# First MLP chunk's second product in seven half-size products, and three changes of order in a transformer block on one core

## The chip, the cores and the metric

The kernel runs on one core of one Trainium2 chip. Its time is device time in microseconds (us). TensorE does the matrix products and writes PSUM; VectorE, ScalarE and GpSimd do the element-wise work; SyncE and GpSimd issue the transfers that are told of here. The profile is one execution taken by the hardware profiler. In it PE is TensorE's matmuls, PEld its weight loads, DVE is VectorE, ACT is ScalarE, POOL is GpSimd, SP is SyncE. [...]

## The reference

One encoder block over 1024 tokens (a grid of 16 rows of 64) and 1024 features, in float32:

```
n = RMSNorm(h);  proj = n @ w_in               (columns: attention q, k, v; GLA q, k, v, r, z)
A = 2-D neighbourhood attention, 8 heads of 64, window 8 x 16, with a bias by relative position
B = bidirectional gated linear attention (GLA), 4 heads, in chunks of 64 tokens; each head's
    output is RMS-normalised and gated by silu(r)
h = h + concat(A, B) @ w_out
h = h + square(relu(RMSNorm(h) @ w1)) @ w2     (w1: 1024 x 4096, w2: 4096 x 1024)
out = RMSNorm(h)
```

## The kernel before, in words

**Layout and parts.** Activations are held with features on the 128 partitions and tokens along the free axis. A float32 product is made of three matmuls: each operand is split into a high part (a cast on ScalarE, `S.copy` to the type float32r) and a low part (the operand less its high part: `low`, line 1057, a subtraction on VectorE or GpSimd), and high x high, high x low and low x high are added up in a PSUM bank of 128x512. Matmuls go out in the order of the program, through `PE`, whose `keep_in_program_order` is at line 115.

**Order of the other engines.** Outside the MLP a scheduler orders the instructions of VectorE, ScalarE and GpSimd by its own estimates and by priorities (`tc.high_priority`), except those kept in program order. In the MLP nearly every instruction is kept in program order (`kp`).

**GLA (lines 440 to 695).** The four heads h = 0 to 3 run one after the other. Between their steps TensorE does the projections of later blocks as filling work: `fill.at(GLA_FILL, h, i)` runs so many steps of three matmuls each. For each half of the 16 token chunks, `gla_contrib` makes eight 64x128 products in two PSUM banks with the tag "s" and copies them to `st`: upper state rows (partitions 0 to 63, line 583) and lower ones (64 to 127, line 586), all four copies of a half on ScalarE. `gla_scan` then runs the recurrence over the chunks on VectorE, forwards on the upper partitions and backwards on the lower ones, one instruction for each step and direction. `gla_within` makes the products inside chunks in two more "s" banks, whose results VectorE copies under a mask (line 600). `gla_intra` and `gla_inter` add up the head's output in a bank "o". `gla_norm` squares it, sums over features with a matmul by ones (bank "t"), and `rstd_from` takes the inverse root with four instructions of ScalarE and two of VectorE; two more of VectorE multiply by the gate and by the output into `yg`. The scan of a head is cut in three: steps 1 to 7 before the first half's `gla_within`, 8 to 11 before the second half's, 12 to 14 behind it.

**Attention (from line 740).** `softmax(p, b, ...)` makes the scores of one pair of heads p and one block of tokens b in two "s" banks, reads them with the bias `bt` on VectorE (line 825), and takes the exponential on ScalarE (827), the reciprocal and the scaling on VectorE (829, 830). `turn` transposes the result on TensorE. The scores of block b + 1 are issued before the transposes of block b, so both banks "s" must have been read by then. `masked` adds masks to the bias on VectorE (771).

**MLP (from line 1040).** The 4096 hidden features are worked off in four chunks of 1024. Each chunk has a first product (w1) and a second (w2), and each product is a list of half-stages of 12 matmuls. `stage` appends half-stages to one list; `go_on` works it off, calling `prepare(k)` ahead of half-stage k. `prepare` issues, in this order: the additions that follow from half-stage k - 1 (`sums`), early sums, the second step of preparing k + 1 (`prep1`), the first step of preparing k + 2 (`prep2`: high and low parts of weights and inputs), late sums, the activation of half-stage k - 1 (`acts`), and the jobs set for k (`job`).

In chunks 1 and 2 both products (`First`, `Second`) are seven products of half-size matrices each, with sums and differences of quarters (Strassen's way in Winograd's form), thus 14 half-stages. Weight sums are called S1 to S4, input sums T1 to T4, quarters A11 to A22 of the weights and B11 to B22 of the inputs; which sums are made where stands in `KW`, `KB`, `FIRST_SUMS` and `SECOND_SUMS`. `Second` takes its inputs' low parts (`lows`) on GpSimd, each pair held back until a first matmul of the half-stage before has run.

In chunk 0 both products are plain: `FirstPlain` and `SecondPlain` have 16 half-stages each. Beside `FirstPlain`, jobs make the second half of the normed activations: `normed` forms a 128x512 block (line 1382) and `put` splits it (cast on ScalarE at 1371, low part on VectorE); the eight blocks come at half-stages 2 to 7. Then `sums123` makes T1 to T3 of the four feature blocks for chunk 1 at half-stages 8 to 15, in the order 1, 2, 3, 0, with GpSimd adding the parts of B11 (`whole`, line 1367), and `sum4` makes T4 in chunk 1. `Weights` loads four quarters of 512 KB on SyncE's queue into four buffers of the tag "raw", each when its buffer is free.

## Time and profile before

| | us |
|---|---|
| median of 3 runs | 1180.3 (1179.51 to 1181.38) |
| profiled execution | 1180.51 |
| its span, first to last instruction | 1178.6 |
| PE busy in the span | 1149.7 (98%) |
| DVE busy | 862.7 (73%) |
| ACT busy | 664.8 (56%) |
| POOL busy | 241.6 (21%) |

The granted clock is 0.990 on average over the span. A record's duration for a pipelined matmul is longer than the distance to the next one; the pace is read from runs of matmuls in the chain of waits. The same holds, less strongly, for VectorE and ScalarE, whose records overlap a little at their ends. In a row of a timeline the bracket gives the idle time ahead of the instruction and what ended it.

### The profile page before, as it was taken

The page shows a single profiled execution, that of the slowest core. Times are in us where ns is not written, and L with a number is a line of the kernel's source. Part 1 is how long each engine was busy: PE and PEld are TensorE (multiplying, and loading weights), DVE is VectorE, ACT ScalarE, POOL GpSimd, SP SyncE. Part 2 cuts the span into 40 slices and gives each one's busy share as a digit, 9 for nine tenths or more (in the row PEclk, how much of TensorE's full clock was granted, in tenths as well). Part 3 has the DMA queues.
Part 4 walks back from the last instruction along what each step waited for, and adds up shares of the span by engine and source line. Part 5 has one row for each costly group of instructions (what it writes and reads, how often), then busy time and mean ns, then how long its engine had stood idle before and what let it go on. Part 6 is the DMA issues. An engine that isn't in the chain of part 4 may idle for free.

```text
span 1178.6 us, 15430 instructions
## 1 busy us (share of the span) xinstructions
PE 1149.7 (98%) x5632; PEld 945.6 (80%) x5632; DVE 862.7 (73%) x1565; ACT 664.8 (56%) x1222; POOL 241.6 (21%) x199
## 2 busy tenths in 40 slices
PE   8999899999999999999999999999999999999996
PEld 8878788767887878887788888888888888888876
DVE  8777868766767785686858875967859768587455
ACT  6767566656666665455634636446355463453665
POOL 5200000202021123510003320402304114032005
PEclk8999999989999999999999999999999999999998
DMA  7333132322324252320211112111211122111204
GB/s 241 76 86 94 41 72 46 87 69 55 80 45 100 68 179 73 107 107 8 82 54 36 54 54 72 37 55 54 72 66 31 50 69 72 54 37 54 72 1 143
DMA packets 40283, 84.03 MB, mean 71 GB/s; under 512 B 9264, under 2 KB 20656, under 8 KB 40208
## 3 DMA queue, kind: packets, MB, share of 16 engines
q1 hardware_dynamic: 36608, 71.11, 18.1%
q0 software_dynamic: 3456, 11.94, 5.8%
q8 instruction: 44, 0.72, 0.2%
q14 instruction: 31, 0.25, 0.1%
q10 hardware_dynamic: 144, 0.00, 0.0%
HBM read 78.85 MB, written 5.96 MB: 72 GB/s over the span
## 4 chain that ended last, share of the span: by engine, by line
PE 83%; DVE 7%; ACT 6%; issue 1%; DMA 1%; SPq 0%; DVEq 0%; ACTq 0%
PE f L115 26%; PE u L115 24%; PE proj L115 15%; PE op L115 7%; PE sc L115 2%; PE no L115 2%; PE o L115 1%; PE pt L120 1%; PE sb L115 1%; PE ob L115 1%; PE z L115 1%; PE a L115 1%; DMA wl<-in_w_in 1%; PE c L115 1%; PE opl L115 0%
## 5 line engine op out<-in xcount | busy, mean ns | idle before, releaser
L1079 ACT CAST ph<-A 128x512 fp32r<-128x512 f32 x166 | 102.9, 621 | 146.5 <-PE f L115 73.6
L1057 POOL TENSOR_TENSOR ul<-uB,uh 128x512 fp32r<-128x512 f32 x84 | 109.1, 1317 | 330.5 <-ACT uh L1092 213.4
L115 PE MATMUL f<-uh,ph 128*128 128x512 f32 x400 | 155.9, 390 | 2.1 <-ACT u L1100 1.4
L115 PE MATMUL f<-ul,ph 128*128 128x512 f32 x400 | 155.8, 390 | 0.1
L115 PE MATMUL f<-uh,pl 128*128 128x512 f32 x400 | 155.8, 389 | 0.0
L1057 DVE TENSOR_TENSOR pl<-A,ph 128x512 fp32r<-128x512 f32 x166 | 112.7, 688 | 52.6 <-ACT ph L1079 52.6
L115 PE MATMUL proj<-nh,wh 128*128 128x512 f32 x352 | 151.1, 429 | 0.0
L115 PE MATMUL proj<-nh,wl 128*128 128x512 f32 x352 | 139.4, 396 | 1.4 <-DMA wl<-in_w_in 1.4
L115 PE MATMUL proj<-nl,wh 128*128 128x512 f32 x352 | 138.9, 395 | 0.0
L1239 DVE TENSOR_TENSOR hT<-hT,f 128x512 f32<-128x512 f32 x168 | 113.0, 687 | 19.8 <-PE f L115 19.6
L115 PEld LDWEIGHTS f<-uh,ph 128*128 128x128 f32 x400 | 75.1, 188 | 18.4 <-ACT u L1100 1.8
L115 PEld LDWEIGHTS f<-ul,ph 128*128 128x128 f32 x400 | 75.1, 188 | 16.0 <-DVE ul L1057 0.4
L115 PEld LDWEIGHTS f<-uh,pl 128*128 128x128 f32 x400 | 75.1, 188 | 15.6
L115 PE MATMUL u<-n,ph 128*128 128x512 f32 x288 | 85.2, 391 | 0.0
L115 PEld LDWEIGHTS proj<-nh,wh 128*128 128x128 f32 x352 | 67.2, 191 | 18.2 <-issue 5.6
L1092 ACT CAST uh<-uB 128x512 fp32r<-128x512 f32 x84 | 51.9, 618 | 51.1 <-PE f L115 33.0
L115 PEld LDWEIGHTS proj<-nh,wl 128*128 128x128 f32 x352 | 66.8, 190 | 16.9 <-DMA wl<-in_w_in 1.8
L115 PE MATMUL u<-T,ph 128*128 128x512 f32 x256 | 77.0, 390 | 0.2 <-ACT ph L1079 0.2
L115 PEld LDWEIGHTS proj<-nl,wh 128*128 128x128 f32 x352 | 67.2, 191 | 11.7 <-issue 1.7
L115 PE MATMUL op<-y,wh 128*128 128x512 f32 x240 | 75.6, 396 | 0.4 <-DVE y L714 0.4
L115 PE MATMUL u<-nt,ph 128*128 128x512 f32 x224 | 69.0, 389 | 0.0
L827 ACT ACTIVATE xsc<-xsc,sm 128x384 f32<-128x384 f32 (+1 forms) x64 | 37.3, 584 | 51.3 <-DVE sm L825 51.1
(302 smaller groups left out, 2469.6 us busy)
## 6 DMA issues: line engine op xcount, KB each, us to landing
A<-in_w SPq DMA_DIRECT2D x64, 512.0 KB
wf<-in_w_in SPq DMA_DIRECT2D x22, 512.0 KB
wl<-in_w_in POOLq DMA_DIRECT2D x21, 512.0 KB, 6.7
wf<-in_w_out SPq DMA_DIRECT2D x17, 512.0 KB
hT<-in_xT SPq DMA_DIRECT2D x2, 2048.0 KB
xs<-in_xT SPq DMA_DIRECT2D x6, 512.0 KB
out<-hT SPq DMA_DIRECT2D x4, 512.0 KB
out<-hT SPq DMA_DIRECT2D x8, 256.0 KB
```

Of the source, the lines that this page charges most:

```text
L115: m = nc.tensor.matmul(*args, **kw)
L120: tc.keep_in_program_order(nc.tensor.transpose(*args, **kw))
L827: S.activation(x[:, :n], x[:, :n], AF.Exp, scale=-1.0, bias=sm[:, i, 0:1], accum_out=sm[:, i, 1:2])
L1057: return kp(eng.tensor_tensor(l, x, h.bitcast(F32), op=ALU.subtract))
L1079: kp(S.copy(ph, x))
L1092: kp(S.copy(uh, x))
L1239: kp(V.tensor_tensor(hT[:, d, c], hT[:, d, c], o[:, s], op=ALU.add))
```

## The change: what it does

1. **Second product of chunk 0.** `SecondPlain` (16 half-stages) goes; chunk 0 uses `Second` as chunks 1 and 2 do (14 half-stages). So `FirstPlain` gets a `late` step that makes T1 (two subtractions on VectorE) and S3 (two weight sums) at its last half-stage. S1 is not made on VectorE: `sum_by_dma` loads A21 from memory into the tile "S" and adds A22 onto it with a second, accumulating transfer, both issued by GpSimd, set as a job at half-stage 9. The first two low parts of the second product's inputs go to VectorE (`eng=V`), without the gate.
2. **Order in the first product of chunk 0.** Low parts are no longer issued right behind their cast. `prep2` and `put` append them to the list `owed`, and `settle` works it off inside the next job, between two other VectorE instructions. The eight normed blocks come at half-stages 2 to 6, `sums123` at 7 to 14 in the order 0 to 3. T1 is formed by subtracting B11's high part and then its low part from B12 (two instructions on VectorE in place of one on GpSimd and one on VectorE), and T2 = B22 - T1.
3. **GLA.** The copies of the lower state rows (line 586) go from ScalarE to VectorE. The scan is cut at 8, 10 in place of 8, 12. For the last head's second half, `gla_norm` is taken apart: the matmul by ones stays where it was, the four ScalarE instructions are issued at the start of attention, and the four VectorE instructions behind the first softmax.

The core of the diff:

```diff
-                S.copy(st[64:128, n0 - 1 + 2 * k:n0 + 6:2, :], src[64:128, k:4, :])
+                V.tensor_copy(st[64:128, n0 - 1 + 2 * k:n0 + 6:2, :], src[64:128, k:4, :])
...
-            gla_scan(dec, st, NCH // 2, NCH - 4)
+            gla_scan(dec, st, NCH // 2, NCH // 2 + 2)
             fill.at(GLA_FILL, h, 4)
             gla_within(h, 1, qD, kI)
-            gla_scan(dec, st, NCH - 4, NCH - 1)
+            gla_scan(dec, st, NCH // 2 + 2, NCH - 1)
...
-            gla_norm(h, 1, ob[1], sq[1])
+            if h + 1 < GH:
+                gla_norm(h, 1, ob[1], sq[1])
+            else:
+                v_last = bank("t", "ovlast")
+                PE.matmul(v_last, ones, sq[1], start=True, stop=True)
+                o_last = ob[1]
...
+        ly = qp.tile([P, T], F32, tag="qc", name="ly")[:, 0:H]
+        lt, lu = qt(), qt()
+        S.activation(lt, v_last, AF.Ln, bias=epsb, scale=LNSH / P)
+        S.activation(ly, lt, AF.Exp, bias=expb, scale=-0.5)
+        S.activation(lu, v_last, AF.Identity, bias=epsn, scale=-0.5 / P)
+        S.activation(lt, ly, AF.Square)
         with tc.high_priority(offset=SOON_B):
             bt = bias_for(0)
         fill.run(NA_PRE)
         xs = softmax(0, 0, *qk, bt)
+        tc.keep_in_program_order(V.tensor_tensor(lt, lt, lu, op=ALU.mult))
+        V.scalar_tensor_tensor(ly, lt, 1.5, ly, op0=ALU.add, op1=ALU.mult)
+        c = slice(H, T)
+        V.tensor_tensor(ly, yg[GH - 1][:, c], ly, op=ALU.mult)
+        V.tensor_tensor(yg[GH - 1][:, c], ly, o_last, op=ALU.mult)
         masked(bt, (5, 0))
...
+        def sum_by_dma(self, dst, a, b, src):
+            self.t[dst] = t = mu.tile([P, D], F32, tag="S", name=dst)
+            kp(G.dma_start(t, src[("A11", "A12", "A21", "A22").index(a)]))
+            kp(G.dma_start(t, src[("A11", "A12", "A21", "A22").index(b)], accum_op=ALU.add))
...
     class FirstPlain(Stage):
+        def late(self, p, kh):
+            if p == (1, 3) and kh:
+                for i in range(2):
+                    t = self.u["B12", i]
+                    kp(V.tensor_tensor(t, t, self.u["B11", i], op=ALU.subtract))
+                for i in range(2):
+                    self.after.w.sum("S3", i)
...
-            self.parts[p, kh] = self.w.low(self.w.high(f"A{p[1] // 2 + 1}{kh + 1}", p[1] % 2))
+            ph, x = self.w.high(f"A{p[1] // 2 + 1}{kh + 1}", p[1] % 2)
+            pl = mp.tile([P, H], F32R, tag="pl", name="pl", bufs=3)
+            self.parts[p, kh] = ph, pl
+            if self.late_lows:
+                owed.append((pl, x, ph))
+            else:
+                low(pl, x, ph, V)
...
+        if isinstance(st, FirstPlain) and get(k + 1)[0] is not st:
+            for n in (k + 1, k + 2):
+                halves[n][0].lows(*halves[n][1:], eng=V)
...
     def put(key, k, x):
         h, l = place(key, k)
         kp(S.copy(h, x))
-        low(l, x, h, V)
+        owed.append((l, x, h))
+
+    def settle():
+        while owed:
+            low(*owed.pop(0), V)
...
         kp(V.scalar_tensor_tensor(t, hT[:, 4 * c + k, H:T], gff[:, 4 * c + k:4 * c + k + 1], r1,
                                   op0=ALU.mult, op1=ALU.mult))
+        settle()
         put(key, k, t)
...
+        h, l = place("B11", k)
         if step == 0:
-            b["B11", k] = ub("b11")
-            whole(b["B11", k], "B11", k)
+            x = ub("t3")
+            kp(V.tensor_tensor(x, b22, b12, op=ALU.subtract))
+            settle()
+            put("T3", k, x)
+            kp(V.tensor_tensor(b12, b12, h.bitcast(F32), op=ALU.subtract))
+        else:
+            kp(V.tensor_tensor(b12, b12, l.bitcast(F32), op=ALU.subtract))
+            settle()
+            put("T1", k, b12)
             kp(V.tensor_tensor(b22, b22, b12, op=ALU.subtract))
-            put("T3", k, b22)
-        else:
-            kp(V.tensor_tensor(b12, b12, b["B11", k], op=ALU.subtract))
-            kp(V.tensor_tensor(b22, b22, b["B11", k], op=ALU.add))
-            put("T1", k, b12)
+            settle()
             put("T2", k, b22)
...
-    f2 = SecondPlain(0, f1.u)
+    f1.after = f2 = Second(0, f1.u)
     stage(f2)
```

## Rows read from the trace of the kernel before

**Rows 1.** The page, parts 1 and 4: busy time by engine; the chain that ended last.

```profile
PE 1149.7 (98%) x5632; PEld 945.6 (80%) x5632; DVE 862.7 (73%) x1565; ACT 664.8 (56%) x1222; POOL 241.6 (21%) x199
...
PE 83%; DVE 7%; ACT 6%; issue 1%; DMA 1%; SPq 0%; DVEq 0%; ACTq 0%
```

**Rows 2.** The chain that ended last: start us, length us, what; x is instructions.

```profile
531.99 7.28 PE u L115 x32
...
582.87 39.09 PE f L115 x171
621.96 38.09 PE u L115 x168
660.05 38.08 PE f L115 x168
```

**Rows 3.** Who TensorE waited for, from 526 to 630 us: total, times, longest.

```profile
PE f L115 <- ACT u L1100: 1.4, 1, 1.4
PE u L115 <- ACT B L1371: 1.0, 1, 1.0
```

**Rows 4.** VectorE in order of time, first product: start us, length us, instructions [idle before].

```profile
535.94 1.29 DVE L1057 TENSOR_TENSOR pl<-A,ph 128x512 fp32r<-128x512 f32 x2
...
541.28 0.69 DVE L1057 TENSOR_TENSOR T<-b,T 128x512 fp32r<-128x512 f32 x1 [0.69 <-ACT T L1371]
541.89 0.75 DVE L1382 SCALAR_TENSOR_TENSOR b<-hT,gff,r 128x512 f32<-128x512 f32 x1
```

**Rows 5.** VectorE, then GpSimd, in order of time, from 725 to 745 us.

```profile
732.01 3.49 DVE L1074 TENSOR_TENSOR S<-A,A 128x512 f32<-128x512 f32 x2
...
737.23 0.68 DVE L1057 TENSOR_TENSOR pl<-A,ph 128x512 fp32r<-128x512 f32 x1
...
731.80 1.45 POOL L1057 TENSOR_TENSOR ul<-uB,uh 128x512 fp32r<-128x512 f32 x1 [38.46 <-ACT uh L1092]
```

**Rows 6.** DMA issues of the page's part 6: KB each, us to landing.

```profile
wl<-in_w_in POOLq DMA_DIRECT2D x21, 512.0 KB, 6.7
```

**Rows 7.** Who TensorE waited for, from 20 to 528 us.

```profile
PE a L115 <- ACT st L586: 1.7, 2, 1.1
...
PE la L115 <- DVE asb L600: 0.8, 1, 0.8
...
PE a L115 <- DVE asb L600: 0.5, 1, 0.5
```

**Rows 8.** Windows: length, busy (and instructions) by engine, granted clock, DMA share, GB/s.

```profile
110.00:160.00 50.00, 46.78 (x260) 37.09 (x260) 37.85 (x65) 31.37 (x49) 2.97 (x5) 0.97 0.30 70
126.00:132.00 6.00, 5.54 (x26) 4.31 (x26) 4.37 (x10) 0.91 (x2) 0.00 (x0) 0.72 0.62 168
256.00:264.00 8.00, 6.95 (x19) 4.87 (x20) 6.22 (x24) 4.82 (x12) 0.86 (x1) 0.57 0.48 93
```

**Rows 9.** VectorE, then TensorE, in order of time, from 236 to 290 us.

```profile
251.31 0.69 DVE L804 TENSOR_TENSOR vT<-proj,rms 128x512 f32<-128x512 f32 x1
252.91 0.69 DVE L239 TENSOR_TENSOR nt<-nt,nu 128x512 f32<-128x512 f32 x1 [0.91 <-ACT nt L238]
...
255.09 0.69 DVE L636 TENSOR_TENSOR yg<-ny,o 128x512 f32<-128x512 f32 x1
...
259.06 0.55 DVE L825 CUSTOM_DVE_ANT_0 xsc<-sc,bt 128x384 f32<-128x384 f32 x1
...
256.85 0.69 PE L115 MATMUL sc<-k00p,q 128*128 128x384 f32 x1 [2.67 <-DVE sm L825]
...
264.39 0.34 PE L115 MATMUL sc<-k00p,q 128*128 128x384 f32 x1
```

**Rows 10.** Groups by line: count, busy us, mean ns, idle before and its releaser.

```profile
L830 DVE TENSOR_SCALAR xsc<-xsc,sm 128x384 f32<-128x384 f32 (+1 forms) x64 | 26.2, 412 | 1.7
...
L888 DVE TENSOR_TENSOR yn<-no,otmp 64x512 f32<-64x512 f32 x16 | 10.9, 682 | 2.3 <-ACT otmp L885 1.8
...
L586 ACT COPY st<-c 64x512 f32<-64x512 f32 (+1 forms) x16 | 8.9, 555 | 0.2
```

More of the change, by code (lines that the diff above doesn't have):

```diff
@@ L692, in block_kernel @@
             fill.at(GLA_FILL, h, 10)
[L693 removed]
+            if h + 1 < GH:
[4 more added lines that the diff above has]
+                o_last = ob[1]
+                assert (h, 1) in gated
         bias_rows(range(ROWS))
@@ L1209, in prep1, with lows @@
                 self.pw[p, i] = self.w.low(self.hw[p, i])
-        def lows(self, p, i, gate=None):
-            self.pu[p, i], op = ulow(self.hu[p, i], G)
+        def lows(self, p, i, gate=None, eng=G):
+            self.pu[p, i], op = ulow(self.hu[p, i], eng)
             if gate is not None:
@@ L1239, in add @@
                 kp(V.tensor_tensor(hT[:, d, c], hT[:, d, c], o[:, s], op=ALU.add))
+    owed = []
     class FirstPlain(Stage):
         order = [((hf, m), kh) for hf in range(2) for m in range(4) for kh in range(2)]
+        late_lows = False
         def __init__(self, c):
             self.w, self.u, self.parts = Weights(w1[c], ("A11", "A12", "A21", "A22")), {}, {}
-        def prep2(self, p, kh):
-            self.parts[p, kh] = self.w.low(self.w.high(f"A{p[1] // 2 + 1}{kh + 1}", p[1] % 2))
+        def late(self, p, kh):
[5 more added lines that the diff above has]
+                    self.after.w.sum("S3", i)
+        def prep2(self, p, kh):
+            ph, x = self.w.high(f"A{p[1] // 2 + 1}{kh + 1}", p[1] % 2)
[5 more added lines that the diff above has]
+                low(pl, x, ph, V)
         def mm(self, p, kh):
@@ L1267, in acts @@
                 relu2(u, self.last)
-    class SecondPlain(Stage):
-        order = [((mh, k), hf) for mh in range(2) for k in range(4) for hf in range(2)]
-        def __init__(self, c, u):
-            self.w, self.u, self.b, self.parts = Weights(w2[c], ("A11", "A12", "A21", "A22")), u, {}, {}
-        def prep2(self, p, hf):
-            mh, k = p
-            if hf == 0:
-                self.wp = self.w.low(self.w.high(f"A{mh + 1}{k // 2 + 1}", k % 2))
-            uu, _ = ulow(uhigh(self.u[f"B{k // 2 + 1}{hf + 1}", k % 2]), V)
-            self.parts[p, hf] = self.wp + uu
-        def mm(self, p, hf):
-            wh, wl, uh, ul = self.parts.pop((p, hf))
-            mh, k = p
-            for j in range(4):
-                if k == 0:
-                    self.b[hf, j] = bank((("o", "t"), ("mm", "s"))[hf][j // 2], f"f{mh}_{hf}_{j}")
-                o = self.b[hf, j]
-                for n, (a, x) in enumerate(((wh, uh), (wl, uh), (wh, ul))):
-                    PE.matmul(o, a[:, j * P:(j + 1) * P], x, start=k == n == 0, stop=k == 3 and n == 2,
-                              skip_group_check=True)
-                if k == 3:
-                    c, d = slice(hf * H, (hf + 1) * H), mh * 4 + j
-                    kp(V.tensor_tensor(hT[:, d, c], hT[:, d, c], o, op=ALU.add))
     halves, jobs, at = [], {}, [0]
@@ L1331, in go_on @@
             else:
-                for t, q in lows:
-                    t.lows(*q)
+                if not isinstance(st, FirstPlain):
+                    for t, q in lows:
+                        t.lows(*q)
                 st.mm(p, i)
@@ L1400, in sum4 @@
         if step == 0:
+            settle()
             b["x", k] = x = [mp.tile([P, H], F32, tag=tag, name=f"b4{k}", bufs=3) for tag in ("uh", "ul")]
@@ L1407, in sum4 @@
             put("T4", k, x[0])
-    for n, k in enumerate((2, 3, 3, 4, 5, 5, 6, 7)):
+    f1.late_lows = True
+    for n, k in enumerate((2, 2, 3, 3, 4, 5, 5, 6)):
         job(k, normed, ("B12", "B22")[n // 4], n % 4)
-    for n, k in enumerate((1, 2, 3, 0)):
-        for step in range(2):
-            job(8 + 2 * n + step, sums123, k, step)
     for k in range(4):
         for step in range(2):
-            job(33 + 2 * k + step, sum4, k, step)
-    f2 = SecondPlain(0, f1.u)
+            job(7 + 2 * k + step, sums123, k, step)
+    job(15, settle)
+    job(9, lambda: f2.w.sum_by_dma("S1", "A21", "A22", w2[0]))
+    for k in range(4):
+        for step in range(2):
+            job(31 + 2 * k + step, sum4, k, step)
+    job(39, settle)
+    f1.after = f2 = Second(0, f1.u)
     stage(f2)
@@ L1421, in block_kernel @@
     stage(f1)
-    go_on(30)
+    go_on(28)
     for c in range(1, nchunk - 1):
```

## The prediction, made blind

> **What bounds the kernel now.** I read the page's busy times first, then the chain that ended last, then TensorE's waits, then the engines in order of time where it waited. TensorE is busy for 98% of the span and holds 83% of the chain [rows 1]. The chain shows its pace: in the MLP 168 matmuls of 512 columns take 38.08 us [rows 2], so one costs 38.08 / 168 = 0.2267 us (the longer durations of single records overlap), and a half-stage of 12 costs 2.72 us. From 621.96 us on, one such block follows the next without a gap. What can be gained is therefore matmuls taken out and waits of TensorE. The waits that this change touches stand in three places: the first MLP chunk [rows 3], the border between GLA and attention [rows 9], and the second GLA head [rows 7]. After the longer waits the granted clock was low as well: 0.57 on average in the 8 us behind the first and 0.72 in the 6 us behind the other [rows 8]. [...]
>
> **First chunk, TensorE.** The second product has 16 half-stages of 12 matmuls now and 14 afterwards: 24 x 0.2267 = 5.44 us less, on the engine that sets the end. The first product's second half-stage starts at 531.99 and the next chunk starts at 621.96 [rows 2]: 89.97 us for 15 + 16 = 31 half-stages, which need 31 x 2.72 = 84.3 us. So 5.6 us are waits, single ones up to 1.4 us [rows 3], the rest short.
>
> **First chunk, VectorE.** The waits come from a pattern. VectorE makes a normed block, ScalarE casts it, and VectorE stands idle for the cast (0.69 us) before it subtracts the low part; only then comes the next block [rows 4]. With the new order the low parts are owed and are done one job later, when their cast is over. I count VectorE's work anew. A 512-column operation costs 0.61 us start to start (two in a row 1.29, less one record of 0.68 [rows 4]), a normed block 0.75 less the same overlap of 0.08, 0.67 us.
> From 536.55 (the first of the pair at 535.94 [rows 4] is done): 8 normed blocks, 5 weight low parts and 7 low parts of the blocks, 8 x 0.67 + 12 x 0.61 = 12.7 us, so 549.2. TensorE needs the last of these at half-stage 9, at 531.99 + 8 x 2.72 = 553.8; now it waits there for the cast. Then, over half-stages 7 to 14: 16 sums, 8 weight low parts and 12 block low parts, 36 x 0.61 = 22.0 us, so 571.2, where TensorE stands at 570.1 (531.99 + 14 x 2.72). This is a balance: nine operations, 5.5 us, for each pair of half-stages of 5.44 us. TensorE waits for none of them, since the sums are for the next chunk and each weight low part comes a half-stage before its use.
> Half-stage 15 then puts seven operations on VectorE: the two first low parts of the second product (they stood on GpSimd in the later chunks), two T1 and two S3 sums, one owed low part, 4.3 us, so 575.5. The first needs of the second product are met (its low parts are done at 572.4, its start is 572.8). Its second half-stage needs a weight low part two operations later, at 576.7, and TensorE wants it with that half-stage's second matmul at 572.8 + 2.72 + 0.23 = 575.7: a wait of about 1.0 us. I take 0.7, since nothing in the count lets VectorE fall back further, and put 0 and 2 us as bounds. From there on it is the later chunks' stage, in which TensorE has no wait [rows 2]: VectorE's additions from PSUM rise from 16 to 28, 12 x 0.61 = 7.3 us more, and with 14 weight low parts and 10 weight and T sums they come to 52 x 0.61 = 31.7 us beside 38.1 us of matmuls.
> Moving those two low parts to VectorE costs 2 x 0.61 and spares a slower pairing: beside GpSimd's low part two weight sums took 3.49 us on VectorE in place of some 1.3 [rows 5].
> Sum for the chunk: 5.4 + 5.6 - 0.7 = **10.3 us** less. Bounds: 11.0 (no wait left) and 4.4 (all old waits stay, plus 1 us).
>
> **One weight sum by DMA.** Two transfers of 512 KB through GpSimd's queue, the second adding onto the first, so it must wait for it: by the rows of such transfers 2 x 6.7 [rows 6] = 13.4 us, a little more with issuing. They can start when the tile that holds block 0 of the normed halves is free, after its last low part at about 556.7, so S1 is there at about 571; ScalarE casts it at about 573 to 575. Behind these transfers on GpSimd stands only the third half-stage's low part, wanted after 575.5. I cost it at nothing. The weights' loads on SyncE's queue, in their new order, wait for the first product's buffers: the last is free at about 568 and, by the same 6.7 us, there at 574.5, before its sum S4 at about 578. If a transfer were late, ScalarE would hold its queue, and TensorE would wait as long.
>
> **Border of GLA and attention.** TensorE runs out at 254.2 and waits 2.67 us until softmax 0 has read its scores [rows 9]. VectorE stood before that in the last head's norm, whose four operations (252.91 to 255.7, after a wait of 0.91 for ScalarE) come ahead of the softmax. Afterwards softmax 0 comes first and can start at 251.9. So the wait at 256.85 goes. What is late next: the four operations now stand between softmax 0 and the masks and scores of softmax 1. VectorE's total to the end of those scores stays, less the idle 0.91 and the short idles around it: 260.0 becomes 259.1 to 259.9. TensorE reaches the third scores at full clock about 4.4 us after 254.2 (12 projection matmuls 2.7, scores 1.0, transposes 0.6), at 258.6, and waits about 1 us. In the trace these scores come at 264.39 [rows 9]: 4.9 us earlier. VectorE's idle time behind it is then used up, and I give back 0.7 us. **4.2 us** less. Bounds: 6.1 (the whole wait and the lost clock) and 0 (the new wait is as long and the clock falls again).
>
> **GLA.** The scan now does two steps rather than four between the halves, so the second half's masks stand four scan instructions earlier: the 0.8 us wait for them [rows 7] goes. Eight pairs of state copies go to VectorE for the lower partitions. On ScalarE each took 0.555 us [rows 10]; the trace has no such copy on VectorE. Nearest rows: 0.682 us (64x512 with an operand in PSUM) above, 0.412 (a scale in SBUF, 128x384) below [rows 10]; I take 0.65, nearest to the first. That is 16 x 0.65 = 10.4 us more for an engine busy 76% here [rows 8], beside 8.9 us less on ScalarE. In the second head TensorE waited 1.7 us for the last of four copies in a row [rows 7], which two engines now share, but a projection's evacuation ahead of them on VectorE moves back by the first pair, and ScalarE's copies behind it. I take half of that and nothing of the clock: 0.8 + 0.7 = **1.5 us** less. Bounds: 4.7 (all three waits, 3.0, and the clock, 1.7) and 3 us more (every head waits 0.75 for the longer VectorE queue).
> [...]
>
> **Sum.** 10.3 + 4.2 + 1.5 = 16.0 us off the profiled execution's 1180.5 (span 1178.6 and 1.9 around it), 1164.5; the median of the runs, 1180.3, is 0.2 below that execution, so 1164.3.
>
> **Rivals.**
> 1. *The border's wait moves, not shrinks.* VectorE has the same work before softmax 1; if TensorE again waits some 2.5 us there and the clock falls, the gain is 0: 1164.3 + 4.2 = 1168.5. For it: VectorE has under 1 us of idle there. Against: half a stage more of TensorE's work is issued before the wait.
> 2. *The first product is bound by VectorE.* Its balance has no slack; if each pair costs 0.7 us more (a cast late, S1 late, GpSimd's issuing in the way), all 5.6 us of waits come back: 1164.3 + 5.6 = 1169.9. That would be the change not doing what its order is for. For it: the count above. Against: no operation in the pair waits for a cast made in the same step.
> 3. *Slower: the GLA copies on VectorE.* The 10.4 us stand on the path of all four heads, whose scans feed the products, and each head's wait takes the clock down for as long as the second head's did, 1.7 us: 10.4 + 6.8 = 17.2 more in place of 1.5 less: 1164.3 + 18.7 = 1183.0. It decides from where VectorE ends a half's two copies later than TensorE has used up the filling projections. For it: VectorE is the busiest engine after TensorE. Against: heads one, three and four now show no wait of TensorE for VectorE or ScalarE above 0.8 us.
> 4. *Everything goes:* 11.0 + 6.1 + 4.7 = 21.8, 1158.5.
>
> **How the numbers follow.** Forecast, all three places gaining, 1160 to 1168: 0.53. Rival 1: 0.17, rival 2: 0.12, rival 3: 0.06, rival 4: 0.12. The range reaches to rivals 4 and 2 with their own spread: 1157.5 to 1173.0, leaving out rival 3 and the ends, about 0.15. A measurement of this kernel tells 0.2%, 2.4 us, from no change. Faster 0.93, same 0.02, slower 0.05: only rival 3 and a sum of two others reach the last two.
>
> **What would show it.** 24 fewer matmuls, and the chunk from 531.99 to the next one's start about 79.7 us long in place of 90.0; no TensorE wait over 1.1 us in it, and the one at the second half-stage of the second product named by a weight low part. No wait of TensorE on softmax 0, one near 1 us for softmax 1, and the clock at 1.00 behind it. VectorE copies near 0.65 us. I am wrong if attention's blocks begin no earlier, if TensorE waits in heads that had no wait, or if the chunk's first product keeps its waits.

## The result, and the profile after

The changed kernel takes 1167.39 us (median of 4 runs, 1167.19 to 1167.57), the kernel before, on the same chip, 1179.9: a ratio of 0.9894 with a 95% interval of 0.9882 to 0.9906, 12.5 us. Forecast were 1164.3 us in a range of 1157.5 to 1173.0, with the largest chance on 1160 to 1168. The profiled execution took 1167.57 us with a span of 1165.8, 12.8 us less than the span before.

First the page of the changed kernel, parts 1 and 4, to be set beside [rows 1]:

```profile
PE 1139.0 (98%) x5608; PEld 939.0 (81%) x5608; DVE 882.0 (76%) x1603; ACT 656.3 (56%) x1210; POOL 253.3 (22%) x209
...
PE 84%; DVE 7%; ACT 5%; DMA 2%; issue 1%; SPq 0%; DVEq 0%; ACTq 0%
```

There are 24 matmuls fewer, as forecast, and TensorE is still the bound. VectorE has 19 us more to do. The chain of waits shows where the MLP's stages begin now (compare [rows 2]):

```profile
527.39 35.39 PE u L115 x156
...
572.18 35.49 PE f L115 x155
607.67 21.77 PE u L115 x96
...
630.64 16.62 PE u L115 x72
647.26 38.08 PE f L115 x168
```

From 562.78 to 572.18 the chain follows VectorE, whose low part ends a wait of TensorE at 572.18. TensorE itself has no break before that wait: its waits in the first product, in [rows 3] before, are no longer listed, and the product's 180 matmuls behind 527.39 end at 568.20. The first chunk's second product ends at 607.67. The second chunk's first product, which was one block of 38.09 us before, is in two pieces with a gap at 629.44. The six largest of TensorE's waits between 40 and 720 us (total, times, longest; compare [rows 3, 7]):

```profile
PE proj L115 <- DMA wl<-in_w_in: 2.4, 2, 1.4
PE c L115 <- DVE st L586: 1.8, 2, 1.0
PE pt L120 <- DVE xsc L836: 1.2, 1, 1.2
PE u L115 <- ACT uB L1195: 1.2, 1, 1.2
PE a L115 <- DVE asb L600: 1.1, 1, 1.1
PE f L115 <- DVE pl L1075: 1.0, 1, 1.0
```

And two of the windows that [rows 8] showed (length, busy by engine, TensorE's granted clock as a share of full speed, DMA share, GB/s):

```profile
126.00:132.00 6.00, 5.24 (x32) 3.83 (x31) 5.62 (x14) 1.04 (x3) 0.40 (x1) 1.00 0.79 176
256.00:264.00 8.00, 6.09 (x30) 4.56 (x31) 6.45 (x20) 2.48 (x10) 0.00 (x0) 1.00 0.60 133
```

The granted clock is 1.00 in both, where before it was 0.72 and 0.57. To see where the 12.8 us are, I cut the span at the same instructions of TensorE in both traces: the first gate product of the first head (51.18 us before, 51.48 after), the last sum of squares of the GLA's outputs that both kernels have (243.21, 242.96), the scores of block 3 in attention (270.83, 266.42), the start of the first MLP product (528.28, 523.68), the start of chunk 1 (621.96, 607.67) and of its second product (660.05, 647.26).

| Stretch | before, us | after, us | gain | forecast |
|---|---|---|---|---|
| up to the first gate product | 51.18 | 51.48 | -0.30 | 0 |
| GLA, four heads | 192.03 | 191.48 | 0.55 | 1.5 |
| border to attention | 27.62 | 23.46 | 4.16 | 4.2 |
| attention and output projection | 257.45 | 257.26 | 0.19 | 0 |
| MLP chunk 0 | 93.68 | 83.99 | 9.69 | 10.3 |
| first product of chunk 1 | 38.09 | 39.59 | -1.50 | 0 |
| the rest | 518.55 | 518.54 | 0.01 | 0 |

The first row is code that all these kernels share; the transfer of the first input stands in it, and it moved between 50.72 and 51.48 us in the runs below. So a difference under 0.8 us between two whole profiled executions is no evidence; I use the lengths of stretches and the medians.

### The profile page after: what moved, and what is told of

Same layout as the page of the kernel before. It is cut to its first block, busy times and chain, and to the rows that moved or that the text cites. A ratio compares the mean times of both kernels' runs of the same rounds, so it can differ in the third digit from the quotient of the medians.

```text
span 1165.8 us, 15400 instructions
## 1 busy us (share of the span) xinstructions
PE 1139.0 (98%) x5608; PEld 939.0 (81%) x5608; DVE 882.0 (76%) x1603; ACT 656.3 (56%) x1210; POOL 253.3 (22%) x209
## 4 chain that ended last, share of the span: by engine, by line
PE 84%; DVE 7%; ACT 5%; DMA 2%; issue 1%; SPq 0%; DVEq 0%; ACTq 0%
PE f L115 26%; PE u L115 25%; PE proj L115 14%; PE op L115 7%; PE no L115 2%; PE sc L115 2%; PE o L115 1%; PE pt L120 1%; DMA wl<-in_w_in 1%; PE sb L115 1%; PE ob L115 1%; DVE st L606 1%; PE a L115 1%; PE z L115 1%; DVE st L586 1%
## 5 line engine op out<-in xcount | busy, mean ns | idle before, releaser
L1075 DVE TENSOR_TENSOR pl<-A,ph 128x512 fp32r<-128x512 f32 x168 | 117.7, 711 | 54.2 <-ACT ph L1103 54.2
L115 PE MATMUL f<-uh,pl 128*128 128x512 f32 x392 | 152.6, 389 | 1.0 <-DVE pl L1075 1.0
L115 PE MATMUL f<-ul,ph 128*128 128x512 f32 x392 | 152.5, 389 | 0.0
L115 PE MATMUL f<-uh,ph 128*128 128x512 f32 x392 | 152.5, 389 | 0.0
L115 PE MATMUL proj<-nh,wh 128*128 128x512 f32 x352 | 149.6, 425 | 0.0
L1263 DVE TENSOR_TENSOR hT<-hT,f 128x512 f32<-128x512 f32 x196 | 131.5, 687 | 22.7 <-PE f L115 22.7
L115 PE MATMUL proj<-nh,wl 128*128 128x512 f32 x352 | 138.3, 393 | 2.4 <-DMA wl<-in_w_in 2.4
L115 PE MATMUL proj<-nl,wh 128*128 128x512 f32 x352 | 137.7, 391 | 0.0
L115 PEld LDWEIGHTS f<-uh,pl 128*128 128x128 f32 x392 | 73.6, 188 | 16.7 <-DVE pl L1075 1.4
L115 PEld LDWEIGHTS f<-uh,ph 128*128 128x128 f32 x392 | 73.6, 188 | 15.4
L115 PEld LDWEIGHTS f<-ul,ph 128*128 128x128 f32 x392 | 73.6, 188 | 15.3
L115 PE MATMUL u<-n,ph 128*128 128x512 f32 x288 | 85.2, 390 | 0.0
L115 PEld LDWEIGHTS proj<-nh,wl 128*128 128x128 f32 x352 | 66.0, 188 | 18.0 <-DMA wl<-in_w_in 3.2
L115 PEld LDWEIGHTS proj<-nh,wh 128*128 128x128 f32 x352 | 66.2, 188 | 17.7 <-issue 5.2
L115 PE MATMUL u<-T,ph 128*128 128x512 f32 x256 | 76.9, 389 | 0.0
L115 PE MATMUL op<-y,wh 128*128 128x512 f32 x240 | 75.7, 396 | 0.4 <-DVE y L720 0.4
L115 PEld LDWEIGHTS proj<-nl,wh 128*128 128x128 f32 x352 | 66.4, 189 | 11.6 <-issue 1.7
L115 PE MATMUL u<-nt,ph 128*128 128x512 f32 x224 | 69.0, 389 | 0.0
L176 POOL DMA_DIRECT2D wl<-in_w_in x21 | 18.4, 878 | 213.6 <-ACT wl L175 153.5
```

The costliest lines, as they stand in the source:

```text
L115: m = nc.tensor.matmul(*args, **kw)
L176: tc.keep_in_program_order(G.dma_start(wl, block, accum_op=ALU.add))
L1075: return kp(eng.tensor_tensor(l, x, h.bitcast(F32), op=ALU.subtract))
L1263: kp(V.tensor_tensor(hT[:, d, c], hT[:, d, c], o[:, s], op=ALU.add))
```

## The experiments

Each kernel is the changed one with a single edit, but for the last, which joins two; each is compared with the 1167.39 us of the changed kernel. Runs had 4 or more timed executions each. They were on several chips; the kernel before, timed beside each, had medians between 1179.53 and 1180.19 us, so a difference of some 0.7 us or less between two medians tells little by itself.

**GLA: copies and scan.** Three edits take the two parts asunder. Heads are counted from 1 here, as in the expectations: head 1 is h = 0 in the code.

```diff
 # copies back on ScalarE, whole
-V.tensor_copy(st[64:128, ...], src[64:128, k:4, :])
+S.copy(st[64:128, ...], src[64:128, k:4, :])
 # scan's cut back, copies stay on VectorE
-gla_scan(dec, st, NCH // 2, NCH // 2 + 2)
+gla_scan(dec, st, NCH // 2, NCH - 4)
...
 # first half's copies on ScalarE, second half's on VectorE
+(V.tensor_copy if hf else S.copy)(st[64:128, ...], src[64:128, k:4, :])
```

> Only the eight pairs of lower state copies go back from VectorE to ScalarE; the scan's new cut, the border's order and the MLP stay as in the changed kernel (1167.4 us). Theory: the copies on VectorE lose about 1.0 us in head 1 (its second half's product waits 0.96 us for a VectorE copy that stands behind other work) and win about 1.2 us or more in head 2, where the granted clock no longer falls. Then this kernel has no such wait in head 1, its second half is at 86.2 us again in place of 87.5, the clock in 126 to 132 us is under 0.9, and the time is 1167.4 to 1168.5. Rival A: the scan's cut alone mended head 2 and the copies only cost; clock 1.00 there, 1166.0 to 1166.6. Rival B: the copies carry all of head 2's gain, about 2.2 us, and more in heads 3 and 4; 1169 or more.

Measured: 1166.2 us (1165.74 to 1166.33), 1.2 us *faster* than the changed kernel. GLA takes 190.29 us in place of 191.48. TensorE's waits there:

```profile
PE a L115 <- ACT st L586: 1.7, 2, 1.1
...
PE a L115 <- DVE asb L600: 0.5, 1, 0.5
```

Of the three waits of [rows 7], that of the gate product (0.8, for line 600) is gone and the one of 1.7 us is back, with the granted clock at 0.72 between 126 and 132 us again. That is the clock which the theory expected and the time of rival A: the scan's cut gains and the copies only cost. Head 1 (from its first gate product to the next head's) takes 39.62 us here and 40.66 with the copies on VectorE, 1.04 us as expected. Head 2 loses only 0.55 without them, low clock included. Heads 3 and 4 together take 0.70 us less without them, though no wait on a copy is listed for them: 0.20 us of it is a wait for a projection's weights (1.44 us there, 1.24 here), the rest short stops.

VectorE in head 1 of the changed kernel shows what the copies stand between:

```profile
76.83 0.69 DVE L471 TENSOR_TENSOR vtmp<-proj,rms 128x512 f32<-128x512 f32 x1
77.55 0.69 DVE L586 COPY st<-c 64x512 f32<-64x512 f32 x1
78.28 2.62 DVE L606 SCALAR_TENSOR_TENSOR st<-st,dec 64x128 f32<-64x128 f32 x7
80.93 1.30 DVE L586 COPY st<-c 64x512 f32<-64x512 f32 x2
```

The first half's copy comes behind line 471, and the second half's products wait 0.96 us for it, where they wait 0.72 for ScalarE's. The second half's two copies then come behind seven scan steps, and the products inside chunks that follow them need their banks: these 16 take 1.76 us from 81.68, in place of 1.16.

> Only the scan's cut goes back to four steps between the halves (the copies stay on VectorE). Theory: the second half's masks stand four VectorE instructions later again, and the wait for them returns in the heads that have no spare filling work, 0.8 to 1.4 us in all: 1168.2 to 1168.8, with a wait on the masked scores in the list of TensorE's waits. Rival: the projections that fill between the halves cover the four instructions, 1167.2 to 1167.6, and the cut is worth nothing by itself.

Measured: 1168.15 us (1168.01 to 1168.97), 0.8 us slower; GLA 192.70 us. One wait comes back:

```profile
136.53 0.50 PE L115 MATMUL la<-zT,guh 128*128 128x512 f32 x1 [0.85 <-DVE asb L600]
```

It is the wait for the masked scores, in head 2 as before, and 0.85 us long. The theory holds, with a time 0.05 us under its range. With both runs the four cases are there: neither edit 192.03, copies alone 192.70, scan alone 190.29, both 191.48. The scan's cut is worth 1.2 to 1.7 us, the copies cost 0.7 to 1.2.

> The lower state copies of a head's first half go back to ScalarE, those of its second half stay on VectorE. Theory: the wait for the second half's scores, 0.96 and 0.82 us in heads 1 and 2, comes from the first half's copy, which stands on VectorE behind the gates' and norm's operations and pushes the second half's copy back; without it both waits go, the clock in head 2 stays at 1.00, and the time is 1166.3 to 1166.7. Rival: what is pushed back is then ScalarE's queue, the same products wait for ScalarE instead by 0.8 us or more, and the time is 1167.4 or above.

Measured: 1165.52 us (1165.28 to 1165.84), 1.9 us faster; GLA 189.39 us. TensorE's waits in heads 1 and 2, in order of time:

```profile
77.57 1.16 PE L115 MATMUL c<-vtok,kt 64*128 64x128 f32 x14 [0.72 <-ACT st L586]
125.45 1.76 PE L115 MATMUL a<-qD,kI 64*128 64x128 f32 x16 [1.28 <-DVE st L586]
131.68 1.13 PE L115 MATMUL a<-qD,kI 64*128 64x128 f32 x14 [1.13 <-DVE asb L600]
```

The gain is larger than the theory's, and its reason only half right: head 1 keeps a wait, of 0.72 us for ScalarE where it had 0.96 for VectorE, but the products that follow are not held up again (16 in 1.17 us), so that the head ends at 90.75, as with all copies on ScalarE (90.66). In head 2 the two halves' copies stand on two engines, one wait of 1.28 us is left of 1.14 and 0.60 (1.7 together in [rows 7]), and the clock is 1.00 between 126 and 132 us.

What one copy costs is in the groups of line 586 between 40 and 245 us (busy, mean ns of one), of the changed kernel and of the one with ScalarE's copies:

```profile
L586 DVE COPY st<-c 64x512 f32<-64x512 f32 x12 | 8.0, 692 | 0.2
```

```profile
L586 ACT COPY st<-c 64x512 f32<-64x512 f32 x12 | 7.0, 581 | 0.2
```

**The border: the last head's norm.** The edit puts the norm of the last head's second half back ahead of softmax 0.

```diff
-            if h + 1 < GH:
-                gla_norm(h, 1, ob[1], sq[1])
...
+            gla_norm(h, 1, ob[1], sq[1])
```

> Only the last head's second norm goes back into GLA, ahead of the first softmax. Theory: its place is the whole of the gain at the border, 4.2 us: TensorE waits 2 to 3 us for softmax 0 again, the granted clock falls in the 8 us behind, and the time is 1171.0 to 1172.0, with the third scores 4 to 5 us later than in the changed kernel. Rival: VectorE's work up to the scores of softmax 1 is the same in either order, and the masks that move into the gaps of softmax 0 or the clock carry the gain; then this kernel loses less than 2 us, under 1169.4.

Measured: 1170.62 us (1170.39 to 1170.95), 3.2 us slower. The border takes 27.17 us in place of 23.46. TensorE's waits there and the window behind:

```profile
255.72 0.45 PE L115 MATMUL sc<-k00p,q 128*128 128x384 f32 x1 [2.69 <-DVE sm L825]
259.59 0.41 PE L120 MATMUL pt<-ident,xsc 128*128 128x128 f32 x2 [1.59 <-DVE sm L829]
264.61 0.50 PE L115 MATMUL proj<-nh,wl 128*128 128x512 f32 x1 [1.14 <-DMA wl<-in_w_in]
...
256.00:264.00 8.00, 5.87 (x26) 3.78 (x25) 6.83 (x25) 4.98 (x14) 0.86 (x1) 1.00 0.62 131
```

The old wait is back in its old size (2.69, before 2.67 [rows 9]), so its cause is the norm's place, as the theory has it, at 3.7 us of the 4.16 by the trace. The clock does not fall, though (1.00 in the window), and the time stays 0.4 us under the theory's range. The kernel before, with the clock at 0.57 in that window, was only 0.45 us longer in this stretch (27.62 against 27.17): as far as these two traces tell, this is what the low clock cost, since here two further waits, for the probabilities and for a projection's weights, stand in its place.

**The waits that are left there.** In the changed kernel the first transposes wait 1.25 us, and a projection then waits 0.92 us for its weights, as none did there in the kernel before:

```profile
256.99 0.41 PE L120 MATMUL pt<-ident,xsc 128*128 128x128 f32 x2 [1.25 <-DVE xsc L836]
...
261.79 0.50 PE L115 MATMUL proj<-nh,wl 128*128 128x512 f32 x1 [0.92 <-DMA wl<-in_w_in]
```

For the first of these, ScalarE in order of time shows what stands ahead (start, length; brackets: idle before):

```profile
253.11 0.51 ACT L833 ACTIVATE xsc<-xsc,sm 128x256 f32<-128x256 f32 x1 [2.71 <-DVE sm L831]
...
253.62 1.04 ACT L175 ACTIVATE wl<-wf 128x1024 fp32r<-128x1024 f32 x1
254.57 1.03 ACT L197 CAST wh<-wf 128x1024 fp32r<-128x1024 f32 x1
255.50 0.50 ACT L833 ACTIVATE xsc<-xsc,sm 128x256 f32<-128x256 f32 x1
```

Two casts of a projection's weights stand between the two exponentials of softmax 0. The edit gives these two exponentials a higher priority.

```diff
+                if (p, b) == (0, 0):
+                    with tc.high_priority(offset=250):
+                        S.activation(x[:, :n], x[:, :n], AF.Exp, ...)
```

> Only the two exponentials of the first softmax get a higher priority on ScalarE, ahead of the two casts of a projection's weights that stand between them in the changed kernel (2.1 us). Theory: TensorE's wait of 1.25 us for the first probabilities goes, but the weights' transfer stands behind one of the casts and starts 0.5 us or more later, so that the wait for those weights grows from 0.92 us to 2.3 to 2.9 us: the border is bound by that transfer, and the time is 1167.2 to 1168.2. Rival: the wait for the probabilities sets the border's end, and the time is 1166.0 to 1166.5.

Measured: 1169.85 us (1168.46 to 1170.15), 2.5 us slower: neither theory. The transposes wait no more, and the weights are no later (0.85 us). But VectorE's order changed with it: with the second probabilities early, all four of the norm's operations went ahead of the second scores of softmax 1, and TensorE waits for these to be read:

```profile
259.15 0.45 PE L115 MATMUL sc<-k10p,q 128*128 128x384 f32 x1 [1.74 <-DVE sm L831]
...
266.09 0.66 PE L120 MATMUL nvt<-ident,vT 128*128 128x128 f32 x4 [0.93 <-DVE pt L867]
```

This is the wait that my prediction had put there. In the changed kernel VectorE takes the norm behind these scores, an order that came with the late exponentials. The border takes 25.12 us in place of 23.46, 1.7 us more. The profiled execution is the fastest of the four; what the median has beyond that, 0.8 us, is in no trace.

**The first product: owed low parts.** The edit makes each low part right behind its cast again, in the new order of the sums.

```diff
 def put(key, k, x):
     ...
     owed.append((l, x, h))
+    if key != "T4":
+        settle()
...
-    f1.late_lows = True
+    f1.late_lows = False
```

> Only the deferral in the first MLP chunk's first product is undone: each low part is made right behind its cast again, of the blocks as of the weights (the owed low parts of T4 in the second product stay as they are, and so does the order of the sums). Theory: the order with owed low parts is what took away the old waits, so they come back, 3 to 5.6 us, and TensorE waits in the first product again behind casts of ScalarE: 1170.4 to 1173.0. Rival: the old waits had other causes (the places of the jobs, the second product's sixteen half-stages) and the deferral is worth under 1 us: 1167.0 to 1168.4, the first product without waits.

Measured: 1182.63 us (1181.85 to 1184.39), 15.2 us slower than the changed kernel and slower than the kernel before, at a ratio of 1.0022 (1.0012 to 1.0031). The direction is the theory's, the size three times its own or more. TensorE's waits from 522 to 720 us, and a window of the first product:

```profile
PE u L115 <- ACT ph L1103: 5.0, 4, 1.9
PE f L115 <- DVE ul L1075: 4.1, 1, 4.1
PE u L115 <- ACT uB L1195: 1.2, 1, 1.2
...
526.00:568.00 42.00, 37.85 (x155) 29.58 (x154) 28.43 (x45) 23.21 (x41) 1.46 (x2) 0.96 0.18 46
```

VectorE is busy for 28.43 of these 42 us; in the changed kernel it is for 38.67. It waits 0.69 us for the cast of nearly every block, as in [rows 4], and the new order has more work for it than the old one, seven operations for the sums of a block where there were six. So it falls ever further back: the second product begins 10 us later (at 582.25 behind its last wait, in the changed kernel at 572.18), waits 4.1 us of them for its first low parts, and the clock is at 0.89 to 0.92 between 552 and 606 us. Owing the low parts does not only take the old waits out, the new order would be a loss without it. Whether owing alone, in the old order and with the old sums, would have done as much was not run.

VectorE in the changed kernel, among the normed blocks as in [rows 4]: a block's low part follows the next block, with no idle time in between.

```profile
540.14 0.68 DVE L1075 TENSOR_TENSOR B<-b,B 128x512 fp32r<-128x512 f32 x1
540.74 0.68 DVE L1075 TENSOR_TENSOR pl<-A,ph 128x512 fp32r<-128x512 f32 x1
541.34 0.74 DVE L1404 SCALAR_TENSOR_TENSOR b<-hT,gff,r 128x512 f32<-128x512 f32 x1
542.00 0.68 DVE L1075 TENSOR_TENSOR B<-b,B 128x512 fp32r<-128x512 f32 x1
```

**The second product: seven or sixteen.** The edit puts the plain second product back; the first product stays.

```diff
-    f1.after = f2 = Second(0, f1.u)
+    f1.after = f2 = SecondPlain(0, f1.u)
...
-    job(9, lambda: f2.w.sum_by_dma("S1", "A21", "A22", w2[0]))
...
-            job(31 + 2 * k + step, sum4, k, step)
+            job(33 + 2 * k + step, sum4, k, step)
```

T4's jobs keep their place by this: the second chunk begins at half-stage 32 here and at 30 in the changed kernel.

> Only the first chunk's second product goes back to sixteen plain half-stages, without the weight sum by DMA and without the sums for it in the first product's last half-stage; the first product's new order stays. Theory: the new form's seven products took 39.5 us and a wait of 1.0 us ahead of them; sixteen half-stages of 2.72 us are 43.5 us, so 3.0 us more, and up to 1.4 us more if the old wait for ScalarE at their start comes back: 1170.4 to 1171.8, 1.2 us less of both if the wait in the next chunk's first product goes as well. Rival: the 24 matmuls are worth their whole 5.4 us and their waits are another matter: 1172.8 or more.

Measured: 1170.05 us (1169.67 to 1171.66), 2.7 us slower. The chain of waits:

```profile
526.93 40.81 PE u L115 x180
567.74 43.53 PE f L115 x192
611.27 38.17 PE u L115 x168
```

Not one wait of TensorE is left in 122 us. From the first product's second half-stage to the next chunk it is 611.27 - 526.93 = 84.34 us, where the forecast for 31 half-stages without waits was 84.3: the new order of the first product takes out all of the old 5.6 us. The wait in chunk 1 is gone too, and that is why the time lies under the theory's main range, within the one 1.2 us lower that it gave for this case. The seven-product form therefore is worth 2.7 us here, not 5.4: the first chunk's second product and the second chunk's first together take 43.53 + 38.17 = 81.70 us in this kernel and 647.26 - 568.20 = 79.06 in the changed one.

**The wait in the second chunk.** It goes with the plain second product, so it comes with the new one (1.21 us up to 630.64, the line `u L115 <- ACT uB L1195` of the list above). Two edits ask how: T4's low parts made at once, or all of T4's steps two half-stages later.

```diff
 # T4 direct
             put("T4", k, x[0])
+            settle()
 # T4 later
-            job(31 + 2 * k + step, sum4, k, step)
-    job(39, settle)
+            job(33 + 2 * k + step, sum4, k, step)
+    job(41, settle)
```

> Only T4's low parts, made during the first chunk's second product, are no longer owed: each follows its cast at once. Theory: the owed low part holds two buffers of the operand tiles past the next step, so GpSimd's last two additions run 3 us later, beside VectorE's operations that they stretch, and from there the next chunk's first product waits 1.2 us for an evacuation on ScalarE; with the low part made at once this wait goes and the time is 1166.0 to 1166.5. Rival: VectorE is behind from the second product itself (its 12 additions from PSUM more), the wait stays at 1 us or more and the time at 1167.1 to 1167.7, or above, since VectorE now waits for four casts.

(In the trace T4's low parts are not made during the first chunk's second product: GpSimd begins with T4's additions there, at 602.84 us in the changed kernel, but VectorE's subtractions and low parts stand between 616.54 and 635.59, in the second chunk's first product.)

Measured: 1166.32 us (1166.18 to 1166.56), as the theory had it, but the wait is not gone:

```profile
629.32 0.73 PE L115 MATMUL u<-B,ph 128*128 128x512 f32 x2 [0.71 <-ACT uB L1195]
```

0.5 us of the 1.2 are the owed parts': GpSimd's last two additions begin at 617.87, in the changed kernel at 620.48, which is 1.8 us sooner counted from the chunk's start (606.85 and 607.67); in both kernels they stand behind a low part of T4. The profiled execution began 0.8 us earlier at the MLP, for nothing that was edited, and from there on gains 0.5 us only, so the median seems to flatter this edit. Both explanations hold a part.

> Only the sums and parts of T4 are made two half-stages later, where VectorE's work of the next chunk's first product is lighter; they stay owed. Theory: the wait of 1.2 us in that product comes from VectorE's lag out of the second product meeting the T4 steps; two half-stages on the lag is worked off and the wait goes: 1166.0 to 1166.5. Rival: the owed low part alone makes it by the two buffers that it holds; the wait only comes two half-stages later, or T4 itself is late for its product, and the time is 1167.1 to 1168.5.

Measured: 1166.06 us (1165.8 to 1166.26). The chain has chunk 1 with a short break only:

```profile
607.17 19.05 PE u L115 x84
...
629.08 16.62 PE u L115 x72
645.70 38.08 PE f L115 x168
```

It takes 645.70 - 607.17 = 38.53 us in place of 39.59, with T4's parts still owed, and of the wait by name 0.15 us is left. VectorE comes into the chunk late (its first low part there stands 2.72 us behind the chunk's start, with the plain second product 1.28), and T4's steps met it there. The seven products alone do not make it late: behind the same form in chunk 1 the first low part stands 686.37 - 685.34 = 1.03 us behind the start of chunk 2. What differs is GpSimd. In the changed kernel it runs T4's first additions from 602.84 us on, and beside them three low parts take VectorE 5.20 us, where two take 1.29 in the next chunk's second product:

```profile
602.87 5.20 DVE L1075 TENSOR_TENSOR pl<-A,ph 128x512 fp32r<-128x512 f32 x3
...
680.54 1.29 DVE L1075 TENSOR_TENSOR pl<-A,ph 128x512 fp32r<-128x512 f32 x2
```

In the kernel before the same additions ran beside VectorE's additions from PSUM, and these were not stretched: four took 2.47 us at 620.85 beside GpSimd and 2.48 at 696.76 with GpSimd idle. This is read from the traces; no run held GpSimd's additions back.

**The wait at the second product's start.** In the changed kernel it is this one:

```profile
572.18 0.50 PE L115 MATMUL f<-uh,pl 128*128 128x512 f32 x1 [1.03 <-DVE pl L1075]
```

The edit puts the wanted low part ahead of the last owed one and of one weight sum.

```diff
-    job(15, settle)
+    job(16, settle)
...
-                (self.w.sum if key[0] == "S" else self.tsum)(key, n)
+                if self.chunk or (key, n) != ("S2", 0):
+                    (self.w.sum if key[0] == "S" else self.tsum)(key, n)
...
             if (p, i) == (1, 0):
+                if not self.chunk:
+                    self.w.sum("S2", 0)
                 self.w.sum("S2", 1)
```

> Only two places in VectorE's order at the border of the first chunk's two products: the last owed low part of the blocks and one weight sum stand behind the low part that the second product's second half-stage wants, in place of ahead of it. Theory: TensorE's wait there (1.03 us, for that weight low part) is two VectorE operations long and goes: 1166.2 to 1166.7, and the second product then ends no later against its start. Rival: VectorE has no slack, the two operations come back as a wait a few half-stages on, and the time stays within 1167.0 to 1167.7.

Measured: 1167.22 us (1166.91 to 1167.32), the rival's. The wait changes its name and place (TensorE, then GpSimd):

```profile
574.85 0.50 PE L115 MATMUL f<-ul,ph 128*128 128x512 f32 x1 [0.89 <-POOL ul L1075]
...
571.59 4.46 POOL L1075 TENSOR_TENSOR ul<-u,uh 128x512 fp32r<-128x512 f32 x2 [13.69 <-PE f L115]
```

Behind the weight low part GpSimd's low part of the third half-stage was late as well: 4.46 us for the two, where the whole kernel's mean is 1.32 for one.

**The weight sum by DMA.** The edit makes S1 on VectorE, in the first product's last half-stage.

```diff
-    job(9, lambda: f2.w.sum_by_dma("S1", "A21", "A22", w2[0]))
...
+                for key in ("S1", "S3"):
+                    for i in range(2):
+                        self.after.w.sum(key, i)
```

> Only the weight sum S1 of the first chunk's second product is made on VectorE again, in the first product's last half-stage, in place of the two transfers. Theory: VectorE has no slack at that border; its two additions, 2 x 0.6 us, stand ahead of the low part that TensorE waits for, so the wait of 1.03 us there grows to about 2.2 us and the time to 1168.3 to 1168.9, and the transfers are free. Rival: the transfers cost GpSimd or ScalarE something near, or the border's wait is set by something else, and the time stays within 1167.0 to 1167.8.

Measured: 1169.1 us (1168.02 to 1169.76), 1.7 us slower. The wait:

```profile
572.83 0.50 PE L115 MATMUL f<-uh,pl 128*128 128x512 f32 x1 [2.21 <-DVE pl L1075]
```

It grew by 1.18 us, two additions, to the size that the theory gave; the second product behind it is longer too (37.02 us in the chain in place of 35.49), which the theory had not, and the time is 0.2 us over its range. The two together are 2.7 us, in the slowest of the four executions; the medians say 1.7. No wait of TensorE for the transfers is listed in the changed kernel.

**Two mends together.** The third edit on the copies and T4 later.

> The two mends that gained by themselves, together: the state copies of a head's first half on ScalarE (1.9 us less than the changed kernel), and T4's sums and parts two half-stages later (1.3 us less). Theory: they lie in different stages and add up, 1164.0 to 1164.6, with no wait of TensorE in the second chunk's first product, none over 1.4 us in GLA, and the scores of softmax 0 some 2 us earlier than in the changed kernel. Rival: time gained in GLA is lost again at the border, whose weights' transfer has its own pace, and the gain is that of the MLP alone, 1165.5 to 1166.2.

Measured: 1164.18 us (1164.01 to 1164.39), a ratio to the kernel before of 0.9866 (0.985 to 0.9883): 3.2 us under the changed kernel. 1.9 and 1.3 add up, as the theory had it.

## Why the prediction was right, and where its sizes were off

The time lies in the range, and within the 1160 to 1168 us that had the largest chance; of the 16.0 us forecast the profiled execution shows 12.8.

**First chunk, 10.3 forecast, 9.7 measured.** The count of VectorE's work held to a few tenths. Shifted by the 4.6 us by which the product began earlier, the count wanted the weight low part between 571.1 and 572.1; TensorE waited from 571.15 to 572.18, by that name. That the two input low parts on VectorE spare a slower pairing on GpSimd was not run by itself. I took 0.7 where the count said 1.0, and 1.03 was right; another 0.36 us are short stops in the second product (568.20 to 607.67 is 39.47 us with the wait, later chunks have 38.08). The old waits went whole, as the plain second product shows.

**A step that failed** is the sentence "From there on it is the later chunks' stage, in which TensorE has no wait". The stage is the later chunks', but what VectorE carries into the next one is not: T4's additions on GpSimd and T4's steps on VectorE exist only there, once, and the sum of 52 operations at 0.61 us has neither them nor the low parts that took 5.20 us for three beside GpSimd. It cost 1.5 us in chunk 1, seen in the changed kernel's chain, gone with the plain second product, and down to 0.45 with T4's steps moved.

**One weight sum by DMA, at nothing.** Right: issued at 551.87 (forecast 556.7 less 4.6) and, after 4.61 us of waiting for the first, at 557.08; its halves were cast at 567.61 and 571.26, and ScalarE waited for neither. On VectorE the sum would have cost 1.7 us.

**Border, 4.2 forecast, 4.16 measured.** The wait on softmax 0 went, by the norm's place: that mechanism is right. The wait of about 1 us behind it came as 1.25 us, but for another reason: ScalarE's weight casts between the exponentials, not the norm ahead of softmax 1. That order exists too, and costs 1.7 us more by the trace and 2.5 by the medians. The 0.7 us that I gave back for VectorE's idle time were lost as well (from the third scores to block 3 it is 7.10 us, before 6.44), but to the 0.92 us wait for a projection's weights, which the prediction does not have. So it is luck that the sum met the measurement to 0.04 us. The 3.4 us for the clock in my bound there, like the 1.7 us in GLA's bound and in rival 3, was an estimate from [rows 8]: their 8 and 6 us times what the granted clock lacks of 1.00 (0.43 and 0.28). No run shows either as time lost. At the border two traces show 0.45 us, since at 1.00 two further waits (1.59 and 1.14 us) fill the time; head 2 at 0.72, with the copies back on ScalarE, is 0.55 us longer in all.

**GLA, 1.5 forecast, 0.55 measured.** The scan's cut was worth more than its 0.8, the copies had the wrong sign: I gave them +0.7 and they cost 0.7 to 1.2. The copy itself, at 0.692 us on VectorE (0.581 on ScalarE), was close to my 0.65. What I left out is the place: a first half's copy on VectorE comes after another operation (0.69 us, line 471) and ahead of the scan, so that the second half's products wait 0.96 us in place of 0.72 and the second half's copies, behind the scan, hold up the next products by another 0.6. I had named that bound (every head loses 0.75 us) and weighed it too low.

**The rivals.** Rival 1 (the border's wait moves) was seen only where the exponentials were put first, with 1.74 us for softmax 1 and no fall of the clock (1.00 from 256 to 264 us). Rival 2 (VectorE binds the first product) is what happens without the owed low parts. Rival 3 had the right direction for the copies, but about 1 us of its 17.2, and no fall of the clock (1.00 from 51 to 243 us). Rival 4 (everything goes) did not come: GLA kept waits, and the border got new ones. The forecast was 3.1 us under the median: 1.0 by GLA, 0.6 by the chunk and 1.5 by chunk 1.

## What to carry to other kernels

When TensorE waits for an engine that itself waits for a cast, owe the dependent step and do it one job later (without that this kernel took 15.2 us more); but count what that engine still carries at the end of the stage, since here it was paid in the next one (1.5 us). When an engine is relieved, ask of each moved instruction what it stands ahead of, not only what it costs: of two equal copies in a head one did better on VectorE and one on ScalarE (GLA 189.39 us so, 190.29 with both on ScalarE, 191.48 with both on VectorE). And matmuls taken out are worth their time only as far as the other engines' work in the stage does not grow: 5.4 us were worth 2.7 here.

## What the runs showed of the chip that I had not expected

The granted clock does not follow from the length of a wait. After a wait of 2.67 us at the border the kernel before had 0.50 from 258 to 262 us, where one projection matmul followed the other by 0.43 us; after one of 2.69 us at the same instruction the kernel with the norm put back had 1.00 and 0.23 us, though its TensorE was busy for less of the time from 250 to 256 us (3.31 us against 4.17). In head 2 waits of 1.14 and 0.60 us came with 0.72 from 126 to 132 us, waits of 1.28 and 1.13 with 1.00. What decides is left open.

And time at low clock is not all lost: in the two traces of the border the stretch with the clock at 0.50 for a time was 0.45 us longer than the same stretch at 1.00 (27.62 and 27.17), which waited elsewhere.
